# First norm of a hybrid decoder layer: queue order of the first loads, roots block by block, third block's squares spread over two rounds

## The chip, the cores and the metric

One core of a Trainium2 chip runs the whole kernel in one launch. The metric is device time in microseconds (us), the median of several runs. Engines are named as in the profile: PE (TensorE, matmuls), PEld (its weight loads), DVE (VectorE), ACT (ScalarE), POOL (GpSimd), SP (SyncE, which issues nearly all DMAs).

## What is computed

One decoder layer and a final norm, for a prompt of 1024 tokens and for 8 sequences of 4 tokens; the width is 1024. Only the head of the layer matters here:

```
mod = silu(c) @ w_ada + b_ada                  # c: 1 prompt row, 8 sample rows; 6 parts of 1024
sh1, sc1, g1, sh2, sc2, g2 = split(mod, 6)
u = rmsnorm(x, norm1_g) * (1 + sc1) + sh1      # rmsnorm: x * rsqrt(mean(x*x) + eps) * g
proj = u @ w_in                                # then SSD heads and S5 groups, w_out, SwiGLU, final norm
```

All is float32 in and out. The big products are made of three products of rounded parts: a high part (`wh`, `uh`) and the rest (`wl`, `ul`).

## The kernel before

The tokens lie along the free dimension, the width in 8 slices of 128 along the partitions. Three blocks of tokens, `BL`, hold 384, 384 and 288 columns; the last has 256 prompt tokens and the 32 sample tokens. A block's input is the tile `xb` of 8 slices (`x_ld`, four DMAs each). The first stage (lines 612 to 705) normalises and modulates all three blocks and multiplies them, slice by slice, with the first two column groups of `w_in` (`raw0`, split into `wh`/`wl` and `wx`/`wl` by `split_h`).

For a block b the steps are:

- `stat_sq(b, k0, k1)` squares slices k0 to k1 on ACT, and DVE and POOL add them into two tiles `acc`, six of the eight slices by addition; at the end DVE adds both.
- `stat_mm(b)` sums over the partitions on PE, `stat_r` takes the reciprocal roots on DVE in twelve small dependent instructions (`rq_m`, `rq_i`, `rq_t`, `rs`), `stat_b` spreads the roots over all partitions on PE and multiplies slice 0 on DVE. ACT copies the spread roots to `rb`.
- For slice k: `prep_a` multiplies by the root (DVE, POOL for block 2), `prep_m` applies the modulation (DVE, ACT for block 1), `prep_h` rounds to `uh` on ACT, `prep_l` takes the rest `ul` (DVE for block 1, else POOL), `u_mm(b, k)` issues six matmuls, `dt_mm` three small ones.
- `ada_do(k, False)` multiplies the conditioning with the modulation weights of slice k (PE, then ACT copies to `adasb`), and `ada_do(k, True)` finishes `mod` for that slice (PE, then two DVE additions and products). `prep_m(b, k)` needs it. The weights come by `ada_ld(k)`, two DMAs of 512 KB each into one of three buffers.

Small parameter arithmetic of the S5 part (about 200 instructions on 128x16 values) is kept in a list, and `s5_ahead(n)` issues the next n of it on DVE (two are on ACT); `stat_r` issues one after each of its twelve steps, `stat_sq` of block 0 three per slice, of block 1 one for each of the first five slices. What is left after the stage goes to the planner, which orders the rest of the program. `warm(n)` issues n matmuls of ones, whose result is not used.

The order within the stage is the order of the code, on PE, DVE, ACT and POOL (`manual_schedule`, line 611); each engine takes its instructions strictly in this order and waits where one is not ready. SP issues DMAs in code order with eight in flight. After `stat_b` of block 1, a loop of ten rounds, k = 1 to 10, handles slice k of blocks 0 and 1 and, three rounds behind, slices of block 2.

Of the kernel before, what the change touches and what calls it, by code (L numbers as in the profile page):

```python
# [45 lines left out]
def build(tc, nc, A, O):  # L46
# [42 lines left out]
    def dma(o, i):  # L89
        if anchor[0] is None:  # L90
            return SY.dma_start(o, i)
        with tc.issue_after(anchor[0].ins):
            return SY.dma_start(o, i)

    def tl(p, shape, tag, dt=F32, bufs=1):
        return p.tile(shape, dt, tag=tag, name=nm(tag), bufs=bufs)

    def ps(shape=(128, 512)):
        return phase["pool"].tile(list(shape), F32, tag="ps", name=nm("ps"), bufs=phase["ps"])
# [4 lines left out]
    def tt(e, o, a, b, op):  # L104
        e.tensor_tensor(o, a, b, op)  # L105
# [10 lines left out]
    def act(o, a, f, bias=0.0, scale=1.0):  # L116
        S.activation(o, a, f, bias=bias, scale=scale)  # L117

    def mm(o, l, r, start=True, stop=True):
        T.matmul(o, l, r, start=start, stop=stop)  # L120
# [145 lines left out]
    def nbt(pt="nb"):  # L266
        return pap.tile([128, 512], F32, tag=pt, name=nm("nb"), bufs=1)
# [68 lines left out]
    def ada_ld(k):  # L336
        raw = tl(xp, [128, 2048], "araw", bufs=3).rearrange("p (k c) -> p k c", k=8)
        for h in range(2):
            m = k + 8 * h
            ld = dma(raw[:, :, 128 * h:128 * h + 128],  # L340
                     A["w_ada"][m // 2].rearrange("p (k c) -> p k c", c=256)[:, :, 128 * (m % 2):128 * (m % 2) + 128])
        AR.append(raw)
        return ld

    def x_ld(b):
        c0, w = BL[b]
        xb = tl(xp, [128, 8, w], f"xb{b}")
        for h in range(4):
            dma(xb[:, 2 * h:2 * h + 2, :], xTv[:, 2 * h:2 * h + 2, c0:c0 + w])
        XB.append(xb)  # L350
# [5 lines left out]
    dma(cst, A["cst"][:, 0:CST1])  # L356
    dma(par2, A["par"][:, PAR1:PARW])
    dma(cst2, A["cst"][:, CST1:CSTW])
    x_ld(1)
    ada_ld(0)  # L360
    raw0 = raw_tile()
    for h in range(2):
        dma(raw0[:, 1024 * h:1024 * h + 1024], A["w_in"][0][:, 1024 * h:1024 * h + 1024])
    dma(wdt, A["wdt"])
    ada_ld(1)
    x_ld(2)
    for k in range(2, 7):
        ada_ld(k)
    anchor[0] = ada_ld(7)
    ast = {}  # L370
# [1 line left out]
    def ada_do(k, fin):  # L372
        if fin:
            pa, sb = ast[k]
            for h in range(2):
                mm(pa[:, 256 + 16 * h:265 + 16 * h], sb[:, 128 * h:128 * h + 128], C["sel"])
            o = pa[:, 256:288].rearrange("p (h r) -> p h r", r=16)[:, :, 0:9]
            d, c, g = mod[:, k:k + 9:8, :], c1[:, k:k + 9:8], P["gs"][:, k:k + 9:8]
            sh = [128, 2, 9]
            tt(V, d, o, c.unsqueeze(2).to_broadcast(sh), add)  # L380
            tt(V, d, d, g.unsqueeze(2).to_broadcast(sh), mult)
        else:
            ast[k] = ada_mm(AR[k], 2)

    def prep_a(b, k):
        c0, w = BL[b]
        xk = XB[b][:, k, :]
        tt(G if b == 2 else V, xk, xk, RB[b], mult)
# [17 lines left out]
    def prep_l(b, k):  # L406
        tt(V if b == 1 else G, U[b][1][:, k, :], XB[b][:, k, :], U[b][0][:, k, :].bitcast(F32), sub)
# [3 lines left out]
    def u_mm(b, k):  # L411
        w = BL[b][1]
        for hh, p in ((0, 0), (0, 2), (1, 0), (1, 2), (0, 1), (1, 1)):
            mm(og[hh, b][:, 0:w], W0[hh][1 if p == 2 else 0][:, 128 * k:128 * k + 128],
               U[b][1 if p == 1 else 0][:, k, :], start=(k == 0 and p == 0), stop=(k == 7 and p == 1))

    def dt_mm(b, k):
        for j in range(3):
            n = 32 if b == 2 and j == 2 else 128
            mm(pd[32 * j:32 * j + 32, 128 * b:128 * b + n], wdt[:, k, :], XB[b][:, k, 128 * j:128 * j + n],  # L420
               start=(k == 0 and b == 0), stop=(k == 7 and b == 2))
# [3 lines left out]
    def stat_sq(b, k0, k1):  # L425
        c0, w = BL[b]
        if k0 == 0:
            sacc[b] = [tl(xp, [128, 384], "acc", bufs=4) for e in range(2)]
        for k in range(k0, k1):
            e = (0, 1, 0, 1, 0, 1, 0, 0)[k]  # L430
            sq_acc(sacc[b][e], XB[b][:, k, :], w, k < 2, (V, G)[e], xp, 4)
            s5_ahead((3, 1 if k < 5 else 0, 0)[b])
        if k1 == 8:
            tt(V, sacc[b][0], sacc[b][0], sacc[b][1], add)

    def stat_mm(b):
        for c in range(3):
            mm(PQ[2][:, 384 + 6 * b + 2 * c:385 + 6 * b + 2 * c], sacc[b][0][:, 128 * c:128 * c + 128], ones[:, 0:1])

    def stat_r(b, n):  # L440
        rs = tl(cp, [128, 9], "rs", bufs=2)[:, 0:3 * n]
        for _ in rsqrt_steps(rs, PQ[2][:, 384 + 6 * b:384 + 6 * b + 6 * n].rearrange("p (c z) -> p c z", z=2)[:, :, 0], 3 * n, 1.0 / 1024):
            s5_ahead(1)
        return rs

    def stat_b(b, rs):
        w = BL[b][1]
        for c in range(3):
            mm(PQ[b][:, 128 * c:128 * c + 128], rs[:, c:c + 1].to_broadcast([128, 128]), ident)
        xk = XB[b][:, 0, :]  # L450
        tt(V, xk, xk, PQ[b][:, 0:w], mult)
        rb = tl(xp, [128, w], f"rb{b}")
        act(rb, PQ[b][:, 0:w], AF.Copy)
        RB.append(rb)
        og[1, b] = ps()

    def warm(n):

        for _ in range(n):
            mm(og[0, 2][:, 0:128], ones, ones)  # L460
# [25 lines left out]
    def s5_ahead(n):  # L486
        for _ in range(min(n, len(SQ))):
            SQ.pop(0)()
# [124 lines left out]
    with tc.manual_schedule(engines=MAN0):  # L613

        V.memset(cs, 0.0)
        act(cs, cs, AF.Silu)
        PQ = [ps() for b in range(3)]
        for b in range(3):
            og[0, b] = psm()
        pd = nbt()  # L620
        for b in range(2):
            stat_sq(b, 0, 8)
            stat_mm(b)
            if b == 0:
                warm(12)
                s5_ahead(10)
        tt(V, c1, P["b_ada"], C["scmask"], add)
        act(cs[:, :, 0:9], P["cT"].rearrange("p (k r) -> p k r", r=9), AF.Silu)
        rs = stat_r(0, 2)
        W0 = [split_h(raw0, 0, V),  # L630
              split_h(raw0, 1, G, (tl(xp, [128, 1024], "wx", F32R), tl(st, [128, 1024], "wl", F32R, bufs=2)))]
        ada_do(0, False)
        stat_b(0, rs[:, 0:3])
        ada_do(0, True)
        prep_m(0, 0)
        prep_h(0, 0)
        stat_b(1, rs[:, 3:6])
        prep_m(1, 0)
        prep_h(1, 0)
        s5_ahead(6)  # L640
        prep_l(0, 0)
        prep_l(1, 0)
        prep_a(0, 1)
        prep_a(1, 1)
        u_mm(0, 0)
        stat_sq(2, 0, 2)
        ada_do(1, False)
        u_mm(1, 0)
        stat_sq(2, 2, 8)
        ada_do(1, True)  # L650
        dt_mm(0, 0)
        dt_mm(1, 0)
        warm(4)
        prep_m(1, 1)
        prep_h(1, 1)
        prep_m(0, 1)
        ada_do(2, False)
        prep_h(0, 1)
        prep_l(1, 1)
        prep_l(0, 1)  # L660
        prep_a(0, 2)
        prep_a(1, 2)
        stat_mm(2)
        ada_do(2, True)
        rs = stat_r(2, 1)
        for k in range(1, 11):
            n, m = k + 1, k - 3
            if k < 8:
                u_mm(0, k)
            if n < 8:  # L670
                prep_m(1, n)
                prep_h(1, n)
                prep_m(0, n)
            if k < 6:
                ada_do(k + 2, False)
            if k < 8:
                u_mm(1, k)
            s5_ahead(12 if k == 1 else 5)
            if k == 1:
                stat_b(2, rs)  # L680
            if 0 <= m + 1 < 8:
                prep_m(2, m + 1)
            if n < 8:
                prep_h(0, n)
                prep_l(1, n)
                prep_l(0, n)
            if k < 8:
                dt_mm(0, k)
                dt_mm(1, k)
            if k < 6:  # L690
                prep_a(0, k + 2)
                prep_a(1, k + 2)
            if 0 < m + 2 < 8:
                prep_a(2, m + 2)
            if 0 <= m + 1 < 8:
                prep_h(2, m + 1)
                prep_l(2, m + 1)
            if k < 6:
                ada_do(k + 2, True)
            if m >= 0:  # L700
                u_mm(2, m)
                dt_mm(2, m)
            if k == 8:

                e0 = tl(cp, [128, 384], "sq", bufs=2)
                act(e0, og[0, 0][:, 0:384], AF.Copy)
                og[0, 0] = e0
# [1427 lines left out]
```

## Time and profile before

| | us |
|---|---|
| median of 3 runs (lowest, highest) | 1280.43 (1278.26, 1291.15) |
| profiled execution, its time | 1284.12 |
| its span, first to last instruction | 1282.3 |
| PE busy in the span | 1220.6 (95%) |
| DVE, POOL, ACT busy | 869.9, 594.9, 533.7 |
| mean granted TensorE clock, share of full | 0.973 |

The profiled execution is 3.69 us above the median. In a timeline each line has the start and the length of a piece in us, the engine, the line of the code, what is written from what, its shape, a count, and in brackets how long the engine had been idle just before and what released it. A float32 matmul appears as two records, so that `x6` stands for three. Since most work is recorded by one helper (line 105 for additions and products, 114 for those with a scalar, 117 for ACT, 120 for matmuls), tiles tell the steps apart: `acc` is a sum of squares, `rs` the roots, `mod` the modulation, `xb` a slice, `uh` and `ul` its parts, `pa` a modulation product, `CP` a table of the S5 part that comes after the stage.

### The profile page before, as it was taken

How to read it: one execution, taken by the hardware profiler on the slowest of the kernel's cores; microseconds unless marked ns; L12 is line 12 of the kernel's file. 1: busy time of each engine (PE TensorE's matmuls, PEld its weight loads, DVE VectorE, ACT ScalarE, POOL GpSimd, SP SyncE). 2: the span in 40 equal slices, each digit the busy share in tenths (PEclk: the TensorE clock that was granted, in tenths of full speed). 3: DMA queues.
4: the chain of work that ended last, by engine and by line, in shares of the span. 5: the costliest groups of instructions: out<-in, count | busy, mean ns of one | idle time of the engine just before them, and what ended most of it. 6: DMA issues, size and time to landing. Idle time of an engine off the chain costs nothing.

```text
span 1282.3 us, 25928 instructions
## 1 busy us (share of the span) xinstructions
PE 1220.6 (95%) x10069; PEld 1155.2 (90%) x10069; DVE 869.9 (68%) x1692; ACT 533.7 (42%) x1102; POOL 594.9 (46%) x544
## 2 busy tenths in 40 slices
PE   4898999999989899999999999999999999999996
PEld 3687788898867799999999999999999999999996
DVE  7898886622478955279866678677776665436775
ACT  4434344444665552354333332333223444434433
POOL 2367961223765442034754555455554444444440
PEclk9999999999978999999999999999999999999997
DMA  9625455456563272721333556465564476656623
GB/s 321 208 65 158 106 128 167 140 160 196 175 210 132 75 240 95 210 73 38 122 126 124 167 167 201 143 208 179 158 199 154 131 255 197 197 184 201 198 100 135
DMA packets 192122, 206.54 MB, mean 161 GB/s; under 512 B 12032, under 2 KB 165120, under 8 KB 186880
## 3 DMA queue, kind: packets, MB, share of 16 engines
q1 hardware_dynamic: 190848, 200.56, 49.9%
q10 hardware_dynamic: 1152, 4.33, 0.8%
q8 instruction: 79, 1.29, 0.4%
q14 instruction: 43, 0.35, 0.1%
HBM read 150.74 MB, written 54.10 MB: 160 GB/s over the span
## 4 chain that ended last, share of the span: by engine, by line
PE 58%; DVE 5%; DMA 2%; issue 1%; ACT 1%; POOL 1%; SPq 0%; ACTq 0%; DVEq 0%; POOLq 0%
PE mm L1567 47%; PE mm L120 9%; PE nb L120 1%; PE ps L120 1%; DMA ar<-w_ada 1%; DVE x L105 0%; DVE v L105 0%; DVE v L114 0%; DVE m L105 0%; DVE arw L105 0%; DMA ts<-hd 0%; DVE m L1525 0%; DMA raw<-w_dn 0%; POOL wh L105 0%; DMA uu<-x2d 0%
## 5 line engine op out<-in xcount | busy, mean ns | idle before, releaser
L1567 PE MATMUL mm<-m,wl 128*128 128x264 f32 x890 | 128.0, 288 | 2.8 <-DVE m L1525 1.7
L1567 PE MATMUL mm<-m,wh 128*128 128x264 f32 x894 | 125.9, 285 | 1.5 <-DVE g L105 0.9
L1567 PEld LDWEIGHTS mm<-m,wl 128*128 128x128 f32 x890 | 117.4, 191 | 3.3 <-DVE m L1525 1.9
L1567 PEld LDWEIGHTS mm<-m,wh 128*128 128x128 f32 x894 | 115.6, 188 | 2.1 <-DVE g L105 1.1
L1567 PE MATMUL mm<-m,wg 128*128 128x264 f32 x771 | 106.3, 286 | 0.0
L1567 PEld LDWEIGHTS mm<-m,wg 128*128 128x128 f32 x771 | 99.6, 189 | 0.0
L105 POOL TENSOR_TENSOR wl<-raw,wh 128x1024 fp32r<-128x1024 f32 x23 | 55.3, 2404 | 92.6 <-ACT wh L117 43.0
L1567 PE MATMUL mm<-m,wf 128*128 128x264 f32 x673 | 92.9, 285 | 0.0
L1567 PEld LDWEIGHTS mm<-m,wf 128*128 128x128 f32 x673 | 86.6, 189 | 0.0
L120 PE MATMUL mm<-uh,wh 128*128 128x384 f32 (+1 forms) x360 | 74.9, 337 | 2.0 <-ACT uh L117 1.9
L105 POOL TENSOR_TENSOR wh<-arw,wh 128x512 fp32r<-128x512 f32 x40 | 55.0, 1374 | 45.2 <-ACT wh L117 45.2
L120 PE MATMUL mm<-uh,wl 128*128 128x384 f32 (+1 forms) x360 | 74.9, 332 | 0.0
L120 PE MATMUL mm<-ul,wh 128*128 128x384 f32 (+1 forms) x360 | 73.5, 330 | 0.7 <-POOL ul L105 0.7
L114 DVE SCALAR_TENSOR_TENSOR xo<-rw,par,xo 128x1024 f32<-128x1024 f32 (+1 forms) x48 | 38.9, 863 | 44.9 <-ACT xo L117 44.9
L120 PEld LDWEIGHTS mm<-uh,wh 128*128 128x128 f32 x360 | 60.4, 191 | 9.3 <-issue 6.4
L105 POOL TENSOR_TENSOR wg<-raw,wg 128x512 fp32r<-128x512 f32 (+2 forms) x31 | 44.1, 1421 | 43.7 <-ACT wg L117 31.1
L105 DVE TENSOR_TENSOR m<-ts,m 128x528 fp32r<-128x528 f32 (+1 forms) x50 | 38.7, 789 | 36.0 <-ACT m L117 35.9
L120 PEld LDWEIGHTS mm<-ul,wh 128*128 128x128 f32 x360 | 59.4, 189 | 3.9 <-issue 2.5
L120 PEld LDWEIGHTS mm<-uh,wl 128*128 128x128 f32 x360 | 60.7, 192 | 1.7 <-issue 1.6
L105 DVE TENSOR_TENSOR arw<-raw 128x512 f32<-128x512 f32 x40 | 43.7, 1094 | 22.5 <-POOL wh L105 15.5
L105 POOL TENSOR_TENSOR wl<-raw,wl 128x512 fp32r<-128x512 f32 (+1 forms) x30 | 41.8, 1394 | 28.5 <-ACT wl L117 28.5
L120 PE MATMUL mm<-m,wh 128*128 128x264 f32 x384 | 54.8, 290 | 0.0
(438 smaller groups left out, 3101.5 us busy)
## 6 DMA issues: line engine op xcount, KB each, us to landing
raw<-w_gu SPq DMA_DIRECT2D x22, 1024.0 KB, 5.3
ts<-hd SPq DMA_DIRECT2D x70, 264.0 KB, 4.0
arw<-w_ada SPq DMA_DIRECT2D x23, 512.0 KB, 4.3
raw<-w_dn SPq DMA_DIRECT2D x11, 1024.0 KB, 5.5
wd<-ts SPq DMA_DIRECT2D x44, 256.0 KB, 2.4
raw<-wd SPq DMA_DIRECT2D x16, 704.0 KB, 4.1
raw<-w_dn SPq DMA_DIRECT2D x12, 704.0 KB, 4.4
araw<-w_ada SPq DMA_DIRECT2D x16, 512.0 KB, 6.2
```

The lines of the kernel that those rows point to most:

```text
L105: e.tensor_tensor(o, a, b, op)
L114: V.scalar_tensor_tensor(o, a, s, b, o0, o1)
L120: T.matmul(o, l, r, start=start, stop=stop)
L1567: T.matmul(o, wv[k][1 if s == 2 else 0], xv[k][1 if s == 1 else 0], start=first and s == 0 and k == 0, stop=(s == 2 and k == n - 1), skip_ ...
```

## The change

The second block of tokens goes behind the modulation weights of slice 0, `raw0` and the weights `wdt` in SP's queue, and the modulation weights of slice 2 go ahead of the third block. The stage first takes block 0 from its squares to its first products, with roots for it alone; only then come the squares, the roots and the first products of block 1. The third block's squares are no longer taken ahead of round 1 but three slices before it and five in it; its roots come at the end of round 1 and are spread in round 2. The numbers of S5 instructions issued ahead are changed, too.

```diff
-    x_ld(1)
     ada_ld(0)
     raw0 = raw_tile()
     for h in range(2):
         dma(raw0[:, 1024 * h:1024 * h + 1024], A["w_in"][0][:, 1024 * h:1024 * h + 1024])
     dma(wdt, A["wdt"])
+    x_ld(1)
     ada_ld(1)
+    ada_ld(2)
     x_ld(2)
-    for k in range(2, 7):
+    for k in range(3, 7):
         ada_ld(k)
...
-        for b in range(2):
-            stat_sq(b, 0, 8)
-            stat_mm(b)
-            if b == 0:
-                warm(12)
-                s5_ahead(10)
+        stat_sq(0, 0, 8)
+        stat_mm(0)
+        warm(12)
         tt(V, c1, P["b_ada"], C["scmask"], add)
         act(cs[:, :, 0:9], P["cT"].rearrange("p (k r) -> p k r", r=9), AF.Silu)
-        rs = stat_r(0, 2)
+        rs = stat_r(0, 1)
+        s5_ahead(6)
...
         ada_do(0, False)
-        stat_b(0, rs[:, 0:3])
+        stat_b(0, rs)
         ada_do(0, True)
         prep_m(0, 0)
         prep_h(0, 0)
-        stat_b(1, rs[:, 3:6])
+        prep_l(0, 0)
+        u_mm(0, 0)
+        dt_mm(0, 0)
+        stat_sq(1, 0, 8)
+        stat_mm(1)
+        rs = stat_r(1, 1)
+        warm(4)
+        stat_b(1, rs)
         prep_m(1, 0)
         prep_h(1, 0)
-        s5_ahead(6)
-        prep_l(0, 0)
         prep_l(1, 0)
+        ada_do(1, False)
         prep_a(0, 1)
         prep_a(1, 1)
-        u_mm(0, 0)
-        stat_sq(2, 0, 2)
-        ada_do(1, False)
+        ada_do(1, True)
         u_mm(1, 0)
-        stat_sq(2, 2, 8)
-        ada_do(1, True)
-        dt_mm(0, 0)
         dt_mm(1, 0)
-        warm(4)
...
         prep_a(1, 2)
-        stat_mm(2)
+        stat_sq(2, 0, 3)
         ada_do(2, True)
-        rs = stat_r(2, 1)
         for k in range(1, 11):
...
-            s5_ahead(12 if k == 1 else 5)
+            s5_ahead(8 if k > 2 else 3)
             if k == 1:
+                stat_sq(2, 3, 8)
+            if k == 2:
                 stat_b(2, rs)
...
             if k < 6:
                 ada_do(k + 2, True)
+            if k == 1:
+                stat_mm(2)
+                rs = stat_r(2, 1)
```

SP's queue, from the last of the parameters on. `xb_13` and `xb_15` are the second block, `xb_17` and `xb_18` the third, `araw` the modulation weights, `raw` is `raw0`:

```order
 L91 DMA cst_2_76<-cst 128x216
-L91 DMA xb_13_100<-xT 128x2x384 x4
-L91 DMA araw_105<-w_ada 128x8x128 x2
-L91 DMA raw_108<-w_in 128x1024 x2
+L91 DMA araw_100<-w_ada 128x8x128 x2
+L91 DMA raw_103<-w_in 128x1024 x2
 L91 DMA wdt_88<-wdt 128x256
+L91 DMA xb_15_107<-xT 128x2x384 x4
 L91 DMA araw_112<-w_ada 128x8x128 x2
-L91 DMA xb_17_115<-xT 128x2x288 x4
-L91 DMA araw_120<-w_ada 128x8x128 x2
+L91 DMA araw_115<-w_ada 128x8x128 x2
+L91 DMA xb_18_118<-xT 128x2x288 x4
```

The second block moves behind 2176 KB of weights, and one more pair of modulation loads stands ahead of the third block.

ACT, from the split of `raw0` on, in the changed kernel. `acc_314` to `sq_338` are the eight squares of block 1, `uh_42` is the first rounded slice of block 0:

```order
L117 ACTIVATE wx_276<-raw_103 128x1024
L117 ACTIVATE adasb_289<-pa_280 128x256
L117 ACTIVATE rb_74_295<-ps_167 128x384
L117 ACTIVATE uh_42_156<-xb_12_91 128x384
L117 ACTIVATE acc_314<-xb_15_107 128x384
L117 ACTIVATE acc_315<-xb_15_107 128x384
L117 ACTIVATE sq_320<-xb_15_107 128x384
L117 ACTIVATE sq_324<-xb_15_107 128x384
L117 ACTIVATE sq_328<-xb_15_107 128x384
L117 ACTIVATE sq_332<-xb_15_107 128x384
L117 ACTIVATE sq_335<-xb_15_107 128x384
L117 ACTIVATE sq_338<-xb_15_107 128x384
```

Before, these eight stood ahead of the split of `raw0`; now they stand behind `uh_42`, which needs the roots and the modulation of block 0.

PE from the warming matmuls (`mm_172<-ones`) on, in the changed kernel. `ps_169<-ones,acc` is `stat_mm`, `ps_167` and `ps_168` are the spread roots of blocks 0 and 1, `pa` is a modulation product:

```order
L120 MATMUL mm_172<-ones_79 128x128 x12
L120 MATMUL pa_280<-araw_100,cs_83 32x256 x8
L120 MATMUL ps_167<-cst_75,rs_238 128x128 x3
L120 MATMUL pa_280<-cst_75,adasb_289 128x9 x2
...
L120 MATMUL nb_173<-xb_12_91,wdt_88 32x128 x3
L120 MATMUL ps_169<-ones_79,acc_314 128x1 x3
L120 MATMUL mm_172<-ones_79 128x128 x4
L120 MATMUL ps_168<-cst_75,rs_345 128x128 x3
L120 MATMUL pa_387<-araw_112,cs_83 32x256 x8
L120 MATMUL pa_387<-cst_75,adasb_396 128x9 x2
```

The sums and the spread of block 1 (`ps_169<-ones_79,acc_314`, `ps_168`) stand behind the first products of block 0; before, its sums stood right behind the warming.

## Rows read from the trace of the kernel before

**Rows 1.** Stretches: PE, PEld, DVE, ACT, POOL busy us, then PE clock, DMA share, GB/s.

```profile
20.00:30.00 10.00, 5.75 (x39) 4.79 (x39) 8.16 (x33) 2.61 (x5) 2.48 (x2) 0.79 1.12 352
...
60.00:84.00 24.00, 24.00 (x221) 18.04 (x220) 21.18 (x74) 9.36 (x19) 13.83 (x16) 1.00 0.17 66
...
110.00:120.00 10.00, 7.38 (x64) 6.47 (x62) 10.00 (x28) 3.44 (x8) 6.36 (x7) 1.00 0.37 100
```

**Rows 2.** DMA issues of the first 75 us: count, KB each, median us to landing.

```profile
xb<-xT SPq DMA_DIRECT2D x8, 384.0 KB, 5.8
...
raw<-w_in SPq DMA_DIRECT2D x2, 512.0 KB, 6.6
```

**Rows 3.** Timeline of ACT: block 1's first squares, and the split of the second half of raw0.

```profile
14.40 0.92 ACT L117 ACTIVATE acc<-xb 128x384 f32<-128x384 f32 x2
...
20.34 1.06 ACT L117 ACTIVATE wx<-raw 128x1024 fp32r<-128x1024 f32 x1 [0.18 <-DMA raw<-w_in]
```

**Rows 4.** Timeline of PE: statistics, warming, modulation, spread of roots, first product.

```profile
13.58 1.44 PE L120 MATMUL ps<-ones,acc 128*128 128x1 f32 x6 [13.58 <-DVE acc L105]
14.88 4.91 PE L120 MATMUL mm<-ones 128*128 128x128 f32 x24
...
21.27 1.07 PE L120 MATMUL pa<-araw,cs 128*32 128x256 f32 x16
25.94 1.65 PE L120 MATMUL ps<-cst,rs 128*128 128x128 f32 x6 [3.59 <-DVE rs L114]
...
29.86 0.69 PE L120 MATMUL mm<-uh,wh 128*128 128x384 f32 x1
...
44.49 0.94 PE L120 MATMUL ps<-cst,rs 128*128 128x128 f32 x6
```

**Rows 5.** Timeline of DVE: sums, roots, first slices and modulations of the stage.

```profile
19.90 0.56 DVE L105 TENSOR_TENSOR acc<-acc,acc 128x384 f32<-128x384 f32 x1
...
21.58 2.29 DVE L248 TENSOR_SCALAR rq_i<-rq_m 128x6 int32<-128x6 int32 x1
...
25.88 1.22 DVE L105 TENSOR_TENSOR wl<-raw,wh 128x1024 fp32r<-128x1024 f32 x1
27.62 0.55 DVE L105 TENSOR_TENSOR xb<-xb,ps 128x384 f32<-128x384 f32 x1 [0.52 <-PE ps L120]
...
29.76 0.55 DVE L105 TENSOR_TENSOR xb<-xb,ps 128x384 f32<-128x384 f32 x1 [0.50 <-PE ps L120]
...
32.49 1.02 DVE L105 TENSOR_TENSOR xb<-xb,rb 128x384 f32<-128x384 f32 x2
...
37.86 0.17 DVE L105 TENSOR_TENSOR mod<-pa,c 128x18 f32<-128x18 f32 x1
...
42.11 0.15 DVE L111 TENSOR_SCALAR rq_m<-ps 128x3 f32<-128x3 f32 x1
...
44.28 0.16 DVE L114 SCALAR_TENSOR_TENSOR rs<-rq_t,rq_i 128x3 f32<-128x3 f32 x1
...
47.07 0.45 DVE L105 TENSOR_TENSOR xb<-xb,ps 128x288 f32<-128x288 f32 x1
...
48.84 0.17 DVE L105 TENSOR_TENSOR mod<-pa,c 128x18 f32<-128x18 f32 x1
...
55.42 0.18 DVE L105 TENSOR_TENSOR mod<-pa,c 128x18 f32<-128x18 f32 x1 [2.43 <-PE pa L120]
```

**Rows 6.** Timeline of POOL: the rest of the second half of raw0.

```profile
21.47 2.37 POOL L105 TENSOR_TENSOR wl<-raw,wx 128x1024 fp32r<-128x1024 f32 x1 [2.84 <-ACT wx L117]
```

**Rows 7.** Timeline of PE after the stage: products that wait for DVE's table CP.

```profile
102.97 0.43 PE L120 MATMUL ps<-CP,BD 128*32 128x128 f32 x8 [0.82 <-DVE CP L105]
...
106.92 0.42 PE L120 MATMUL ps<-CP,BD 128*32 128x128 f32 x8 [1.04 <-DVE CP L114]
...
120.11 0.42 PE L120 MATMUL ps<-CP,BD 128*32 128x128 f32 x8 [2.72 <-DVE CP L114]
```

## The prediction

> **What bounds the kernel now.** I read the stretches first, then the timelines of the engines in the first 60 us, then TensorE's waits behind the stage. TensorE is busy for 95% of the span, so time can be won only where it has nothing to do or runs slowly, and the largest such place is the head. There it has no real product before 29.86 us: it waits 13.58 us for block 0's squares, warms, then waits 3.59 us for the roots [rows 4]. The stretch from 20 to 30 us shows it busy for 5.75 of 10 us at a granted clock of 0.79, a mix of the two levels 1.2 and 2.4 GHz, while the DMA engines move 352 GB/s without a pause [rows 1]. From 60 to 84 us TensorE is busy in all 24.00 us and VectorE in 21.18: the rounds are then TensorE's. From 110 to 120 us it is the reverse, VectorE busy in 10.00 of 10 and TensorE in 7.38 [rows 1].
>
> What the reader is to see in the head is a chain over four engines. The two blocks' squares end together at 19.90 + 0.56 = 20.46 us, one chain of roots serves both, and from then on block 0 and block 1 go side by side. The modulation of slice 1, which opens the rounds, is on VectorE at 37.86; the next two that I follow are at 48.84 (slice 3) and 55.42 (slice 4) [rows 5]. I use these three as milestones, since everything of a round waits for its modulation.
>
> **Loads.** A piece of block 1 is 384 KB, a half of `raw0` 512 KB [rows 2]. Before, the second half of `raw0` lands just ahead of 20.34, where ScalarE waits for it [rows 3]. In the new queue the last piece of block 1 has the same bytes ahead of it and the 128 KB of `wdt` besides: 131 KB (thousands) at 352 GB/s are 0.4 us, so it lands at 20.7. The second half of `raw0` has four pieces less ahead of it, 1.57 MB or 4.5 us, and lands at 15.9. The loads of slice 1's weights keep their place; those of slice 2 come earlier and the third block 1 MB (3.0 us) later, by the same rate at about 30 us, while its squares are now wanted after 40. So no load is on the path, and I cost the reordered queue at nothing. Its cover is ScalarE's order (below); without it, block 1 could start 20.7 us at the earliest, against 14.40 before [rows 3].
>
> **Block 0 alone, a gain.** Its squares and sums are unchanged: `stat_mm` runs from 13.58 to 15.02. A chain of roots without a stall is 42.11 to 44.28 + 0.16, that is 2.33 us with its S5 instructions between [rows 5], so the roots are there at 17.4. In the chain before, one instruction took 2.29 us beside a VectorE-blocking GpSimd split of 2.37 us [rows 5, 6]; this stall goes, because the split now starts only at about 18.3 (ScalarE's two halves of 1.06 us each follow a sine that waits for the root chain's sixth S5 instruction at 16.2). The split may hold up VectorE's own split of 1.22 us until 20.7, which then ends at 22.0. But TensorE is no sooner: the warming holds it until 14.88 + 4.91 = 19.8, the modulation product (1.07) until 20.9, the spread at full clock (0.94) until 21.8 [rows 4]. So VectorE multiplies slice 0 at 22.1 with or without the stall. From that step to the first product it was 29.86 - 27.62 = 2.24 us [rows 4, 5]; the first product starts at 24.3, 5.5 us earlier than before.
>
> **Block 1 behind it, a loss.** ScalarE takes block 1's squares behind `uh` of block 0, so not before 24.3, though the data were there at 20.7. From first square to last sum it was 14.40 to 20.46, 6.06 us [rows 3, 5]: 30.4 now. Then `stat_mm`, roots 2.33, spread, and from slice 0's product to the end of the two `prep_a`, 29.76 to 32.49 + 1.02, 3.75 us [rows 5], after which slice 1's modulation comes. For `stat_mm` and the spread I must choose a clock. TensorE has nothing but 3 us of work between 22 and 30 us. Before, a wait of 3.59 us was followed by a spread of 1.65 us instead of 0.94 [rows 4], so I take the slow values, 1.44 and 1.65; the floor is 0.7 us less for the spread and 0.6 for the sums. With 0.2 for four hand-overs: 30.4 + 1.44 + 2.33 + 1.65 + 3.75 + 0.2 = 39.8, against 37.86: **+1.9 us**, bounds +0.6 and, should the two blocks' GpSimd additions delay each other by one more 1 us, +2.9.
>
> The Trainium skill (TensorE: Matmul & The Clock Gate, Part 1) says that the slow clock is the default and that activity releases it; the slow spread behind the wait of 3.59 us [rows 4] agrees. By that rule alone the four extra warming matmuls ahead of block 1's spread could bring it back to full, and the step would be +1.2 instead of +1.9.
>
> **Third block's squares.** Before, they filled VectorE from 33.51 to slice 1's modulation at 37.86, 4.35 us [rows 5]. They are the reason why block 1's delay costs only 1.9 us, and they are not gone: they come between the modulations of slices 1 and 3, which took 48.84 - 37.86 = 10.98. Out of that stretch go the third block's roots (2.33), its first product (0.45) and most of twelve S5 instructions (44.44 to 47.07, with one other instruction of about 0.45 in it: 2.2); into it come the squares (4.35) and six S5 instructions (0.6 to 1.2 at 0.1 to 0.2 each, the root chain's 24 instructions in 2.33 us being 0.1 each). 10.98 - 4.98 + 4.95 = 10.95: no change. Then from slice 3 to 4, 6.58 us before: in come roots and product, 2.78, and VectorE had been idle for 2.43 there, waiting for TensorE [rows 5], which hides most: +0.35. So slice 4's modulation stands at about +2.2 us, and the rounds behind it are TensorE's and carry this on.
>
> **S5 instructions.** The head now issues 15 more (three chains of roots instead of two, +12; the fixed counts -10; the rounds 70 instead of 57, +13). In rounds 3 to 10 there are 24 more, 2.4 to 4.8 us of VectorE spread over a stretch in which it had 2.8 to spare [rows 1]: nothing, or up to 2 us. What is issued early is missing behind: 15 times 0.1 to 0.2 is 1.5 to 3 us less on VectorE where TensorE waits 0.82 + 1.04 + 2.72 = 4.58 us for it [rows 7]. I give back 1 us, between 0 and 2.2. Behind the stage the planner has shuffled matmuls up to about 300 us; no row prices that, and I put it at ±2 us, half of the 4.58 us of waits that it can touch here.
>
> **Sum.** +1.9 + 0.3 - 1 = about +1.2, rounded up to +1.5 for the fuller rounds. The profiled execution would take 1285.6 instead of 1284.12; that execution is 3.69 us above the median, so I add to the median: **1282 us**.
>
> **Rivals.**
> (1) Block 0's lead survives. If ScalarE and GpSimd get through block 1's squares much faster than 6 us, or if the rounds had slack enough to take the third block's squares for nothing, TensorE's earlier start of 5.5 us is kept: 1275. For it: TensorE has real work 5.5 us sooner. Against it: the rounds need both blocks and the modulations, and VectorE has little idle time between 38 and 52 us.
> (2) Slower, by the clock. TensorE now has three holes in a row, before block 1's sums (26 to 30), during its roots (32 to 34) and during its preparation (36 to 38). If the granted clock stays at the lower level from 30 to 50 us, the products there take twice as long: the spread went from 0.94 to 1.65. Some 13 us of TensorE work lie in that stretch, and about half has no cover: +6, 1287. It decides itself where the clock of 30 to 50 us falls below 0.8; with the 0.79 of 20 to 30 us before [rows 1] that is near.
> (3) The change does not do what it says: GpSimd's split at 18 to 21 us and VectorE's two-input work block each other for longer, so that block 0 is no earlier than 27. Then all of block 1 follows 3 us later still: 1285.
>
> **Chances and range.** Forecast (1279 to 1285) 0.52, rival 1 0.22, rival 2 0.18, rival 3 0.08. A gain or loss of 1% is 12.8 us, about what a measurement of this kernel can tell from no change; it would take two of these together or a shuffle behind the stage of ten microseconds. Faster by over 1% 0.05, within 1% 0.88, slower 0.07. The range takes in rivals 1 and 2 with the planner's ±2 and 1 more for the median's own scatter: 1272 to 1290.
>
> **What would show it.** In the profile of the changed kernel: the first product (`mm<-uh,wh`) at 24.3, not 29.9; ScalarE's `acc<-xb` of block 1 right behind `uh` at 24; a second chain of roots from about 32; slice 1's modulation at 39.8 (rival 1: 33 or earlier; rival 2: the same, but with a clock under 0.8 until 50); slice 4's at 57 to 58; waits for `CP` shorter than 4.58 us in sum. I am wrong if block 1's sums end well before 30 us, or if the difference arises behind 125 us, in the shuffled part.

## The result: 1.2% slower, and the profile after

| | before | after |
|---|---|---|
| median (lowest, highest), 11 runs each | 1282.88 (1277.71, 1291.15) | 1295.30 (1291.72, 1305.56) |
| profiled execution, its time / span | 1284.12 / 1282.3 | 1293.09 / 1290.9 |
| mean granted TensorE clock of the runs | 0.975 (29 runs, shared with later comparisons) | 0.969 (11 runs) |

The ratio is 1.0117, 95% interval 1.0096 to 1.0138: some 15 us slower (12.4 us between the medians), against a forecast of +1.5 us. The time lies outside the range.

The same stretches of the changed kernel, in the columns of [rows 1]:

```profile
20.00:30.00 10.00, 4.32 (x40) 2.88 (x33) 7.28 (x17) 4.81 (x11) 3.32 (x3) 0.83 1.13 357
...
60.00:84.00 24.00, 23.06 (x216) 17.27 (x219) 23.07 (x71) 10.27 (x20) 12.70 (x14) 1.00 0.22 87
...
110.00:120.00 10.00, 8.38 (x63) 7.21 (x62) 10.00 (x24) 2.29 (x6) 8.00 (x13) 1.00 0.42 115
```

From 60 to 84 us the roles have changed: TensorE has gaps, and VectorE, which had 2.8 us to spare, is now busy for 23.07 of 24 us. The next lines, on wider stretches of the changed kernel, let the loss be added up. TensorE's idle time is the stretch less its busy time, and what the clock costs is about the busy time times what the clock lacks to 1.

```profile
0.00:20.00 20.00, 7.08 (x38) 6.76 (x42) 13.75 (x61) 8.23 (x16) 4.71 (x7) 1.00 0.94 322
20.00:60.00 40.00, 28.24 (x216) 19.72 (x208) 28.13 (x104) 16.15 (x37) 10.02 (x10) 0.83 0.71 212
60.00:110.00 50.00, 46.01 (x374) 37.77 (x375) 48.32 (x176) 21.07 (x48) 31.05 (x57) 1.00 0.27 93
110.00:225.00 115.00, 105.76 (x802) 90.98 (x801) 96.59 (x181) 41.31 (x84) 73.26 (x104) 0.93 0.52 138
225.00:420.00 195.00, 183.58 (x1532) 155.99 (x1531) 106.71 (x190) 108.42 (x238) 90.29 (x91) 0.97 0.54 170
```

The kernel before in the same stretches:

```profile
0.00:20.00 20.00, 6.21 (x30) 6.02 (x30) 13.79 (x50) 10.66 (x23) 4.57 (x8) 1.00 0.92 311
20.00:60.00 40.00, 31.70 (x256) 22.84 (x257) 32.80 (x127) 16.24 (x36) 11.66 (x11) 0.87 0.76 231
60.00:110.00 50.00, 48.14 (x382) 40.64 (x381) 46.92 (x161) 20.08 (x48) 33.70 (x63) 1.00 0.32 106
110.00:225.00 115.00, 108.25 (x869) 94.08 (x868) 89.90 (x185) 46.34 (x92) 68.81 (x99) 0.99 0.52 142
225.00:420.00 195.00, 184.51 (x1487) 158.52 (x1486) 110.41 (x189) 105.14 (x234) 91.20 (x90) 0.92 0.53 166
```

TensorE is idle for 0.9 us less up to 20 us, 3.5 us more from there to 60 us (11.76 against 8.30), 2.1 more from 60 to 110 us and 2.5 more from 110 to 225 us. There the clock adds 105.76 x 0.07 = 7.4 us against 1.1. From 225 to 420 us it is the other way, 5.5 against 14.8; that profile of before had a low clock there (0.92; the sixteen other traces have 0.93 to 0.97). The two profiles are 8.6 us apart where the medians are 12.4. Over its whole span the profiled change has a clock of 0.974, and before 0.973, and TensorE is busy for as long as before:

```profile
PE 1220.7 (95%) x10069; PEld 1152.1 (89%) x10069; DVE 882.1 (68%) x1704; ACT 533.5 (41%) x1102; POOL 596.4 (46%) x544
```

So of the 8.6 us between these two executions 8.5 are idle time (70.2 us against 61.7). The clock's part of the loss does not show in this pair; it shows in the runs' mean clock, 0.969 against 0.975.

The head of the changed kernel on TensorE, where [rows 4] stood:

```profile
23.61 0.44 PE L120 MATMUL mm<-uh,wh 128*128 128x384 f32 x1 [1.67 <-ACT uh L117]
...
29.56 1.44 PE L120 MATMUL ps<-ones,acc 128*128 128x1 f32 x6 [3.89 <-DVE acc L105]
30.86 2.06 PE L120 MATMUL mm<-ones 128*128 128x128 f32 x8
33.53 1.62 PE L120 MATMUL ps<-cst,rs 128*128 128x128 f32 x6 [0.62 <-DVE ta L105]
```

And on VectorE, where [rows 5] stood:

```profile
28.95 0.56 DVE L105 TENSOR_TENSOR acc<-acc,acc 128x384 f32<-128x384 f32 x1
...
38.87 0.17 DVE L105 TENSOR_TENSOR mod<-pa,c 128x18 f32<-128x18 f32 x1
...
45.83 2.97 DVE L105 TENSOR_TENSOR acc<-acc,sq 128x288 f32<-128x288 f32 x3 [1.37 <-ACT sq L117]
...
50.78 0.17 DVE L105 TENSOR_TENSOR mod<-pa,c 128x18 f32<-128x18 f32 x1
...
56.04 0.45 DVE L105 TENSOR_TENSOR xb<-xb,ps 128x288 f32<-128x288 f32 x1 [1.48 <-PE ps L120]
57.65 2.44 DVE L105 TENSOR_TENSOR xb<-xb,rb 128x384 f32<-128x384 f32 x2
60.01 0.17 DVE L105 TENSOR_TENSOR mod<-pa,c 128x18 f32<-128x18 f32 x1
```

The modulations of slices 1, 3 and 4 stand at 38.87, 50.78 and 60.01, that is +1.0, +1.9 and +4.6 us against [rows 5]. Between the last two the third block's first product waits for the spread of its roots, and two root products take 2.44 us, which took 1.02 [rows 5]. On GpSimd there is then one instruction behind the other:

```profile
57.42 1.18 POOL L105 TENSOR_TENSOR ul<-xb,uh 128x384 fp32r<-128x384 f32 x1 [8.94 <-ACT uh L117]
58.56 1.11 POOL L105 TENSOR_TENSOR xb<-xb,rb 128x288 f32<-128x288 f32 x1
59.63 1.11 POOL L105 TENSOR_TENSOR ul<-xb,uh 128x288 fp32r<-128x288 f32 x1
```

The Trainium skill (SBUF — State Buffer, section "SBUF: two separate sides") says that a VectorE instruction with two SBUF inputs and a GpSimd instruction that reads SBUF shut each other out for a whole instruction. These rows agree: 1.4 us were lost next to GpSimd's three.

Behind the stage, the products that wait for the table `CP`, where [rows 7] stood:

```profile
111.89 0.43 PE L120 MATMUL ps<-CP,BD 128*32 128x128 f32 x8
116.25 0.43 PE L120 MATMUL ps<-CP,BD 128*32 128x128 f32 x8 [1.10 <-DVE CP L114]
...
130.12 0.66 PE L120 MATMUL ps<-CP,BD 128*32 128x128 f32 x8 [3.13 <-DVE CP L114]
```

The last one is 10.0 us later than in [rows 7]; it is the milestone "last CP" below.

### The profile page after: what moved, and what is told of

Read it like the earlier page. It is cut to its first block, busy times and chain, and to the rows that moved or that the text cites. A ratio compares the mean times of both kernels' runs of the same rounds, so it can differ in the third digit from the quotient of the medians.

```text
span 1290.9 us, 25933 instructions
## 1 busy us (share of the span) xinstructions
PE 1220.7 (95%) x10069; PEld 1152.1 (89%) x10069; DVE 882.1 (68%) x1704; ACT 533.5 (41%) x1102; POOL 596.4 (46%) x544
## 4 chain that ended last, share of the span: by engine, by line
PE 72%; DVE 16%; ACT 3%; DMA 3%; issue 3%; POOL 2%; SPq 0%; ACTq 0%; DVEq 0%; POOLq 0%
PE mm L1570 45%; PE mm L120 18%; PE ps L120 5%; PE pa L120 1%; PE nb L120 1%; DVE tp L105 1%; DVE xb L105 1%; ACT m L117 1%; DVE Ec L114 1%; DVE h L105 1%; DMA ts<-hd 1%; DVE gf L105 1%; DVE acc L105 1%; DVE m L105 1%; DVE ta L105 1%
## 5 line engine op out<-in xcount | busy, mean ns | idle before, releaser
L114 DVE SCALAR_TENSOR_TENSOR xo<-rw,par,xo 128x1024 f32<-128x1024 f32 (+1 forms) x48 | 35.9, 803 | 39.5 <-ACT xo L117 39.5
```

The source lines that it names most:

```text
L114: V.scalar_tensor_tensor(o, a, s, b, o0, o1)
```

## Experiments

Three theories were put up. A: the loss is made in the stage, by the third block's squares and by eight S5 instructions a round. B: by TensorE's clock in the head. C: by the planner's other order behind the stage. D, E and F came later. All fifteen runs follow; slices 1 and 4 are the modulations, `Vq` is ScalarE's first copy in the S5 part, and the clock is that of 110 to 225 us:

| run | ratio (95%) | slice 1 | slice 4 | last CP | first Vq | clock |
|---|---|---|---|---|---|---|
| before | 1 | 37.9 | 55.4 | 120.1 | 117.0 | 0.99 |
| the change | 1.0117 (1.0096 to 1.0138) | 38.9 | 60.0 | 130.1 | 132.7 | 0.93 |
| a_sq2 | 1.0104 (1.0063 to 1.0144) | 38.7 | 55.9 | 126.1 | 128.7 | 0.91 |
| a_s5 | 1.0073 (1.0050 to 1.0097) | 38.5 | 63.4 | 127.7 | 125.6 | 0.96 |
| b_sq2 | 1.0006 (0.9981 to 1.0030) | 34.8 | 56.5 | 122.4 | 119.3 | 0.97 |
| b_s5 | 1.0039 (1.0009 to 1.0070) | 38.6 | 55.3 | 124.7 | 126.8 | 0.91 |
| a_sq2_s5 | 1.0051 (1.0025 to 1.0077) | 38.8 | 60.1 | 124.6 | 121.9 | 0.91 |
| a_warm | 1.0103 (1.0063 to 1.0143) | 38.5 | 59.6 | 129.5 | 132.1 | 0.85 |
| a_queue | 1.0123 (1.0089 to 1.0157) | 39.7 | 62.3 | 131.5 | 134.1 | 0.93 |
| b_s5_2 | 0.9987 (0.9965 to 1.0010) | 36.6 | 53.3 | 115.4 | 112.1 | 0.97 |
| a_dah | 1.0130 (1.0092 to 1.0169) | 39.0 | 61.7 | 131.0 | 127.4 | 0.93 |
| b_s5_dah | 1.0044 (1.0019 to 1.0070) | 36.1 | 51.4 | 120.4 | 117.1 | 0.85 |
| h_par | 1.0089 (1.0057 to 1.0121) | 41.0 | 61.0 | 125.8 | 123.1 | 0.99 |
| b_vs2 | 0.9967 (0.9943 to 0.9990) | 36.1 | 52.8 | 114.6 | 111.5 | 0.97 |
| a_fill | 1.0089 (1.0060 to 1.0118) | 39.1 | 60.2 | 134.8 | 137.0 | 0.96 |
| b_s5_fill | 1.0024 (1.0005 to 1.0043) | 36.7 | 51.1 | 124.5 | 126.8 | 0.94 |
| b_vs5 | 0.9972 (0.9944 to 1.0000) | 34.8 | 52.1 | 116.9 | 113.7 | 0.96 |

Each trace is one execution; the ratios are of all runs, against the runs of before made beside them. How far single traces scatter is seen in b_s5, b_s5_dah and b_s5_fill: their code is the same up to slice 4, which comes at 55.3, 51.4 and 51.1. So a difference of 4 us between the milestones of two traces shows nothing by itself. That the new order has slice 4 late holds over its traces (59.6 to 63.4, and 55.9 in a_sq2, against 51.1 to 56.5).

### Parts of the change, undone or done alone

a_sq2 (against the change), and b_sq2 (the third block's squares and roots of the change, on the kernel before). In a_sq2 the squares stand ahead of round 1 again, but behind the modulation of slice 1; in the kernel before they stand ahead of it, too:

```diff
         dt_mm(1, 0)
+        stat_sq(2, 0, 8)
...
-        stat_sq(2, 0, 3)
+        stat_mm(2)
         ada_do(2, True)
+        rs = stat_r(2, 1)
...
             if k == 1:
-                stat_sq(2, 3, 8)
-            if k == 2:
                 stat_b(2, rs)
...
-            if k == 1:
-                stat_mm(2)
-                rs = stat_r(2, 1)
```

> The change, but with the third block's squares and roots where they were before, ahead of round 1 and spread in round 1. Theory A (the loss is made in the stage: about 3 us in rounds 1 to 4 by the third block's squares, 2 to 4 in the last rounds by eight S5 instructions a round, and both are carried on): slice 3's modulation moves back from 50.8 to 52 us at most, slice 4's comes at 57 instead of 60.0, the time is 3 us below the change's, 1.008 of before. Theory B (TensorE's clock): slice 4's modulation stays at 60, since the clock in 40 to 60 us stays at 0.91; 1.012. Theory C (the planner's other order behind the stage makes the loss): slice 4's modulation may move, the time stays within 1.010 to 1.014.

> The kernel before, with the third block's squares and roots in rounds 1 and 2 as in the change, and nothing else. Theory A: slice 1's modulation comes 3 to 4 us sooner (37.9 to about 34), slice 4's is 0 to 3 us later than before (55 to 58), the time 1.000 to 1.003. Theory B: 1.000. Theory C: 1.000 or 1.01, without a delay in the stage.

a_s5 (against the change) and b_s5 (the reverse, on the kernel before):

```diff
-            s5_ahead(8 if k > 2 else 3)
+            s5_ahead(12 if k == 1 else 5)
```

> The change, but with the numbers of S5 instructions in the rounds as before (12, then 5 a round, instead of 3, 3, then 8). Theory A: nothing moves up to slice 4's modulation or it comes up to 1 us later, the three waits of 0.5 to 1.3 us in the last rounds go, the first square of the second norm's sums (97.8 us) comes 2 to 4 us sooner, the time is 3 us below the change's, 1.009. Theory B: 1.012. Theory C: the time follows the planner's order and not the stage's end: any value from 1.000 to 1.015, whatever the stage's end does.

> The kernel before, with the change's numbers of S5 instructions in the rounds (3, 3, then 8). Theory A: slice 4's modulation is 0 to 1 us sooner, the first square of the second norm's sums (89.4 us) 2 to 4 us later, the time 3 us above before, 1.002. Theory B: 1.000. Theory C: any value from 0.995 to 1.010, whatever the stage's end does.

a_sq2_s5 has both undone, so that the order block 0, then block 1, and the queue are left:

> The change with the third block's squares and roots and the numbers of S5 instructions in the rounds both as before; what is left of it is the order block 0, then block 1, and the reordered queue. Theory A (S5 counts cost 4 to 7 us, the serial head some 3, the third block's squares little): slice 1's modulation at 38.5 to 39, the last product of the S5 table ahead of the planner's part (130 us in the change, 120 before) at 122 to 124, time 1.003 to 1.005. Theory B (a lower clock in the head makes most of it, because TensorE is idle between the blocks): time 1.006 to 1.010 and a mean clock of 0.970 as in the change. Theory C (planner): any value, whatever that product does.

Undone one after the other, the parts are: order and queue 1.0051; with the squares 1.0073, hence 1.0022 for them; with the S5 counts 1.0117, hence 1.0044. A third pair differs by the counts, a_sq2 and a_sq2_s5: 1.0104 against 1.0051. On the other side the S5 counts alone give 1.0039 and the squares alone 1.0006. In us: 6.5 for the order (3 to 10 by its interval), 5 to 7 for the counts (1 to 9 by that of b_s5), 1 to 3 for the squares, whose sign no interval settles. Theory A has the parts, but its milestones were wrong. In a_s5 the last CP is only 2.5 us sooner than in the change and slice 4 is 3.4 later, yet the time falls. In b_sq2 the last CP comes 2.3 us later than before, for nothing.

What the order does, with the squares behind slice 1, is seen on VectorE in a_sq2_s5:

```profile
38.84 0.18 DVE L105 TENSOR_TENSOR mod<-pa,c 128x18 f32<-128x18 f32 x1
45.52 0.16 DVE L105 TENSOR_TENSOR mod<-pa,c 128x18 f32<-128x18 f32 x1
52.74 0.17 DVE L105 TENSOR_TENSOR mod<-pa,c 128x18 f32<-128x18 f32 x1
60.05 0.18 DVE L105 TENSOR_TENSOR mod<-pa,c 128x18 f32<-128x18 f32 x1 [3.33 <-PE pa L120]
```

Slice 1 is late by 1.0 us only, but slices 3 and 4 by 3.9 and 4.6: the third block's squares, which stood ahead of slice 1 before (4.35 us by the prediction's own reading of [rows 5]), now come behind it.

On TensorE the price of the order stands in the head itself. From 20 to 60 us the eight traces with the new order and no more warming have 10.3 us of idle time in the mean, and the clock costs 7.5; the six with the order of before and GpSimd's split have 6.6 and 5.2. That is 6 us, of which 2 are the clock's.

The queue (a_queue: `x_ld(1)` back ahead of `ada_ld(0)`, `x_ld(2)` ahead of `ada_ld(2)`):

> The change with the queue of before: block 1 ahead of the first modulation weights and raw0, the third block ahead of the weights of slice 2. The prediction's term (the reordered queue costs nothing): block 0's first product stays within 0.5 us of 23.6, or is up to 1 us later because the second half of raw0 lands at 20.3 instead of 15.9; the time stays as it is, 1.010 to 1.013. The rival: block 0's lead comes from the queue, the first product falls back to 26 or later.

Its first product comes 0.8 us later (24.40), the time is that of the change. The term was right: the new queue costs nothing, and brings next to nothing.

a_warm, against the change:

```diff
         dt_mm(0, 0)
+        warm(12)
         stat_sq(1, 0, 8)
...
-        warm(4)
+        warm(8)
```

> The change with more warming matmuls of ones: twelve more between block 0's first products and block 1's sums, where TensorE is idle for 3.9 us, and eight instead of four during block 1's roots. Theory A: the sums take 0.8 instead of 1.4 us, the spread 0.9 instead of 1.6, slice 1's modulation comes 1 to 1.5 us sooner (37.4 to 37.9), the time falls by 1 to 2 us, 1.010. Theory B: the clock stays at the upper level from 20 to 45 us in every run, the mean clock of the runs goes from 0.969 back to about 0.974, the time falls by 5 us, 1.007. If the warming runs at the lower clock it holds TensorE until 32 us and the time rises by 2.

```profile
20.00:60.00 40.00, 30.79 (x253) 23.03 (x256) 29.27 (x107) 16.15 (x37) 11.19 (x11) 0.91 0.76 233
```

The head's clock went from 0.83 to 0.91, but slice 1 came only 0.4 us sooner, and slices 3 and 4 by the same 0.4 (50.36 and 59.57). So the clock in the head is not what holds these milestones. That it costs no time is not shown: the interval, 1.0063 to 1.0143, leaves room for B, and the traced execution is the slowest of its six.

h_par, an attempt to find the price within the order: a_sq2_s5 with the queue of before and

```diff
         stat_mm(0)
         warm(12)
+        stat_sq(1, 0, 8)
...
         dt_mm(0, 0)
-        stat_sq(1, 0, 8)
         stat_mm(1)
```

> The change with the queue, the third block's squares and the S5 counts of before, and with block 1's squares right behind block 0's; what is left of the change is that roots, spread and first product of block 0 come ahead of the roots of block 1. Theory A (block 1's squares behind block 0's products are what delays the rounds, since VectorE stands idle meanwhile): VectorE is busy for at least 29 of the first 40 us (26.3 in the change, 29.5 before), slice 4's modulation is back at 55 to 56.5, time 1.000 to 1.002, against 1.005 with the squares behind. The rival (the separate roots, one chain more, cost it): slice 4's modulation at 58 or later, 1.004 to 1.006.

```profile
28.92 0.69 PE L120 MATMUL mm<-uh,wh 128*128 128x384 f32 x1 [1.93 <-ACT uh L117]
...
31.71 1.44 PE L120 MATMUL ps<-ones,acc 128*128 128x1 f32 x6
...
35.69 1.62 PE L120 MATMUL ps<-cst,rs 128*128 128x128 f32 x6 [0.62 <-DVE ta L105]
```

Theory A's reason falls. With early squares block 1's sums still stand behind block 0's products in TensorE's order, and sums, roots and spread come as a second chain, 31.71 to 37.31, with VectorE busy for only 23.93 of the first 40 us, not 29. The early squares make block 0 late as well, and the time is no better than that of a_sq2_s5. This fits the rival, that the second chain in series costs the time, and slice 4 is late as it says (61.0); but the ratio lies above the rival's 1.006, too, and no run sets the two chains side by side, so the reason stays argued.

### Why eight S5 instructions a round cost 5 us

b_s5_2, the kernel before with `s5_ahead(12 if k == 1 else 2)`:

> The kernel before with two S5 instructions instead of five in each of rounds 2 to 10, so 27 fewer ahead of the planner's part. Theory A (VectorE has room for five in a round and not for eight; what does not fit in a round is paid behind it): the stage ends 0 to 1 us sooner than before, but the 27 are then paid where VectorE is busy without a pause, 84 to 120 us: +2 to +4 us at the last table product, time 1.001 to 1.003. Theory C (the planner's order decides): any value from 0.995 to 1.006, without relation to the stage's end.

The expected price of 2 to 4 us did not come. All milestones are sooner, slice 4 by 2.1 us and the last CP by 4.7, for 1.7 us or nothing of time.

a_dah and b_s5_dah, the change and b_s5 with

```diff
-    act(dAh, dA, AF.Copy)
+    V.tensor_copy(dAh, dA)
```

since in the change ScalarE stands as follows, where before `Vq` came first:

```profile
132.56 0.26 ACT L117 ACTIVATE dAh<-dA 128x72 fp32r<-128x72 f32 x1 [9.18 <-DVE dA L105]
132.73 0.66 ACT L117 ACTIVATE Vq<-ps 128x272 f32<-128x272 f32 x2
```

> The change, but the small copy dAh (128x72, of a VectorE result) is made by VectorE and not by ScalarE. In the change ScalarE stands 9.2 us in front of it, and the first Vq copy, whose product has been ready for 5 to 6 us, stands behind it in ScalarE's order; in the kernel before the Vq copy comes ahead. Theory D (this order is how the S5 counts cost 5 to 6 us): the first Vq copy comes at about 127 instead of 132.7, the time falls to 1.007 to 1.008. Theory E (VectorE's work up to the last table product is what counts, the copy's place is hidden): the first Vq copy comes sooner, but the time stays at 1.010 to 1.013.

> The kernel before with the change's numbers of S5 instructions (1.0039 by itself) and dAh made by VectorE. Theory D: first Vq copy at about 122 instead of 126.8, time back to 0.999 to 1.001. Theory E: 1.003 to 1.005.

D falls in both: the first `Vq` copy comes 5.3 and 9.6 us sooner, and the time stays. E's numbers come out, but not its reason: in b_s5_dah the last CP is at 120.4, as before, and the time is 1.0044 all the same. The traced execution itself took 1289.78 us, 5.7 more than that of before. So the price is behind these milestones. The stretch from 110 to 225 us of b_s5, then of b_s5_dah:

```profile
110.00:225.00 115.00, 106.19 (x791) 91.17 (x790) 93.32 (x184) 42.09 (x85) 68.74 (x102) 0.91 0.50 132
```

```profile
110.00:225.00 115.00, 107.04 (x755) 91.38 (x754) 87.48 (x166) 39.89 (x78) 64.76 (x91) 0.85 0.49 130
```

And of a_s5, which has before's counts:

```profile
110.00:225.00 115.00, 107.03 (x823) 93.28 (x824) 97.28 (x194) 39.06 (x84) 70.59 (x105) 0.96 0.50 135
```

In all seven traces with the change's counts and nothing put into the waits the clock is 0.85 to 0.93 there; in seven of the eight with five or two a round it is 0.96 to 0.99 (the eighth, a_sq2_s5 with 0.91, comes from the slowest of its twelve runs; but among the seven the 0.85 of a_warm comes from the slowest of its six, too). TensorE's busy time hardly differs, 105 to 108 us against 106 to 109. From 0.97 to 0.90 is 106 x 0.07 = 7 us, the size that is sought. Part of it comes back later: over whole executions the seven have a mean clock of 0.970 and the eight 0.973, some 4 us. To test it, a_fill and b_s5_fill issue the first half of the second group's products with `CP` seven times, ahead of the wait (3.13 us in the change):

```diff
-        for r in range(2):
+        for i, r in enumerate(([0] * 7 if q == 1 else [0]) + [1]):
...
-                   CP[:, r, t, 0:8].rearrange("p j c -> p (j c)"), start=(r == 0), stop=(r == 1))
+                   CP[:, r, t, 0:8].rearrange("p j c -> p (j c)"), start=(r == 0), stop=(r == 1 or q == 1 and i < 6))
```

> The change with 24 more small matmuls in TensorE's order just ahead of its wait for the second group's last S5 table (3.1 us at 130 us): the first half of that group's products is issued seven times instead of once. Theory F (TensorE's clock falls behind its waits there, and this is the S5 counts' price): with the wait filled the lower clock takes under 10 us of the stretch 110 to 225 instead of 17, the time falls by 3 to 5 us, 1.008 to 1.009. Theory C (the planner's order behind the stage is worse by itself): the clock may rise, the time stays at 1.011 to 1.013. If the planner moves other products in front of the wait, TensorE may wait for those instead and nothing is told.

> The kernel before with the change's S5 counts (1.0039) and the same 24 matmuls ahead of the wait of 2.8 us at 125 us. Theory F: lower clock between 110 and 225 under 10 us instead of 20, time 1.000 to 1.002. Theory C: 1.003 to 1.006.

The planner did what the expectation feared. In a_fill TensorE now waits for other products:

```profile
132.74 0.91 PE L120 MATMUL nb<-dA,cst 128*128 128x64 f32 x10 [5.64 <-DVE dA L105]
```

Still the clock of the stretch rose (0.93 to 0.96, 0.91 to 0.94), and the ratios went from 1.0117 to 1.0089 and from 1.0039 to 1.0024, though their intervals overlap. The fall owes much to the runs of before: their median is 1284.14 in this comparison and 1282.1 to 1282.9 in the others. The medians of a_fill and b_s5_fill, 1297.53 and 1288.08, are no lower than the change's 1295.30 and hardly lower than the 1288.94 of b_s5.

The mean clock of all runs says how much of the counts' price the clock can be. In the change it is 0.969, in a_s5 0.973, which is 5 us, nearly the whole difference. In b_s5 it is 0.972 against 0.975 before, 3 of 5 us; in a_sq2 0.970 against the 0.971 of a_sq2_s5, 1 of 7. With the fills it is back, 0.973 and 0.9765 against 0.973 before, but the time is not, 1.0089 where a_s5 has 1.0073, and 1.0024 where it should be 1; the fills add TensorE work and, in a_fill, a new wait. So the clock is a part of how the counts cost time, and that it is the whole is not shown; why the planner's order with these counts loses the clock stays open.

### A version faster than both

b_vs2 and b_vs5: the kernel before, with the second half of `raw0` split by VectorE; b_vs2 also has the counts of b_s5_2.

```diff
-              split_h(raw0, 1, G, (tl(xp, [128, 1024], "wx", F32R), tl(st, [128, 1024], "wl", F32R, bufs=2)))]
+              split_h(raw0, 1, V, (tl(xp, [128, 1024], "wx", F32R), tl(st, [128, 1024], "wl", F32R, bufs=2)))]
```

> An attempt at a better version: the kernel before with two S5 instructions instead of five in rounds 2 to 10, and the second half of raw0 split by VectorE instead of GpSimd. If GpSimd's split is what stalls one instruction of the root chain for 2.3 us, the first modulation comes 1 us sooner, VectorE pays 1.2 us for the split; the time 0.997 to 0.999. If the stall has another cause, the chain stays and the split is added: 1.000.

> The kernel before with only the second half of raw0 split by VectorE, S5 counts as before. If the removed stall of 2.3 us in the root chain brings the gain of b_vs2 (0.9967), the first modulation comes at 26 to 27 and the time is 0.997 to 0.999; if the fewer S5 instructions bring it, 1.000.

In b_vs5 the instruction that took 2.29 us beside GpSimd's split [rows 5, 6] takes 0.17, and the first modulation is at 25.73 instead of 28.35:

```profile
20.82 0.17 DVE L248 TENSOR_SCALAR rq_i<-rq_m 128x6 int32<-128x6 int32 x1
...
22.99 1.22 DVE L105 TENSOR_TENSOR wl<-raw,wh 128x1024 fp32r<-128x1024 f32 x1
24.13 1.22 DVE L105 TENSOR_TENSOR wl<-raw,wx 128x1024 fp32r<-128x1024 f32 x1
```

b_vs2 is faster than before, 0.9967 (0.9943 to 0.9990), some 4 us; b_vs5, 0.9972, differs from it by nothing that these runs resolve, so the gain most likely comes with the split. That the shorter root chain brings it is not shown: the runs' mean clock is 0.977 in both, against 0.974 and 0.973 in the runs of before beside them, which is 4 and 6 us, as much as the gain. The change, too, took this stall out of the root chain, as forecast; its other parts cost more than that brings.

## Why the prediction was wrong

- **Loads and block 0: right.** First product at 23.61, forecast 24.3; the queue is neutral (a_queue).
- **Block 1: right up to its milestone, wrong in what it costs.** Slice 1 came at 38.87, inside the bounds, with the slow sums (1.44) and the slow spread (1.62) that were chosen, in spite of the four warming matmuls between them. But the +1.9 was taken as the price of the order, and the order with the queue costs 1.0051, 6.5 us (3 to 10). The step that failed is to price the order by VectorE's milestone alone: TensorE's idle time and clock from 20 to 60 us, where the new order loses some 6 us, were not summed.
- **Third block's squares: a second step that failed in the head.** "10.98 - 4.98 + 4.95 = 10.95: no change" and "+0.35" let the rounds take 4.35 us of VectorE for nothing. (Of these, 0.74 us were VectorE's waits for ScalarE's squares at 34.26 and 34.93.) Slice 3 was 0.9 us and slice 4 3.6 us later than slice 1's own delay. The stretch was summed as if VectorE alone had to be fed; the 2.43 us of idle time that were to hide the rest [rows 5] went, and 1.48 of waiting for the spread, 1.4 beside GpSimd and, ahead of slice 3, 1.37 of waiting for ScalarE's squares (45.83) came. Against the milestone's forecast of about 57.6 (+2.2) this is 2.4 us. What it costs in time stays open: b_sq2, the same move on the kernel before, costs nothing that is resolved (1.0006). Moving the squares back in the full change brings slice 4 4.1 us sooner, but the time recovers little (a_sq2, 1.0104).
- **S5 counts: the term with the largest error.** "nothing, or up to 2 us" in the rounds is about what the rounds show (TensorE idle from 60 to 110 us 2.52 in b_s5 against 1.86). "I give back 1 us", with "±2" for the planner, was the mistake: instead of a gain the counts cost 5 to 7 us, and by the traces most of it behind the stage, between 110 and 225 us, where the prediction had no row but the three waits [rows 7]. It had named this as a sign of being wrong (a difference behind 125 us). These became 4.23 us in sum (1.10 + 3.13), hardly shorter than 4.58.
- **Rival 2, the clock: right in part, and not only where it was looked for.** In the profiled change the clock from 30 to 50 us is 0.83 and back by 40 us, and holding it there gave nothing that is resolved (a_warm). But six of the eight traces with the new order have 0.55 to 0.71 there, under the rival's 0.8, where the kernel before has 0.93 and its seven variants 0.74 to 0.98; it costs some 2 us of the forecast 6. It is low later, too: the runs of the change have 0.969 in the mean against 0.975, and among them the time goes with it, 1291.72 us at 0.974 and 1305.56 at 0.962. By this pair 0.006 is 7 us, about half of the loss.
- Rival 1 fell, as block 0's lead of 6.25 us was gone by slice 1; rival 3 did not occur.

## What to carry to other kernels

Follow the work of the engine that is short, here VectorE, to a milestone that needs all of it: work moved past an early milestone makes that one look cheap and is paid at the next. Where a planner orders what comes after, a change in the amount of work handed to it has a price of its own that no milestone in the stage shows; measure such a part alone before it is bundled. And where TensorE is 95% busy, add up idle time and lost clock by stretches; here, from 110 to 225 us, the clock's part grew by 6.3 us and the idle time by 2.5. Add up to the end, too, since another stretch can give it back (225 to 420 us, 9.3 us), and compare the mean clock of all runs before a mechanism is read from one trace.

## Not expected of the hardware

- The times of one kernel's runs follow their mean granted clock: 12 runs of b_sq2 go from 1279.53 us at 0.979 to 1288.70 at 0.970. Two kernels that differ by less than that can be told apart only by many runs.
- A GpSimd split holds a tiny VectorE instruction for its whole length, one with a single input, too: `rq_i` (128x6) took 2.29 us before, `tb` (128x16, two inputs) 2.35 us in b_s5, each next to a split of some 2.36 us, and 0.17 us for `rq_i` with the split gone.
